# Large tiles on multiples of 512 bytes, and one of eight pairs of row blocks multiplied plainly, in a transformer layer's up projection

## The chip, the core and the metric

The kernel runs on one core of a Trainium2 chip. A core has five engines, each with its own queue of instructions: TensorE (PE: multiplications, and PEld: the loads of their stationary operand), VectorE (DVE), ScalarE (ACT), GpSimd (POOL) and SyncE (SP), which in this kernel issues nearly all DMAs. On-chip memory is SBUF, 128 partitions wide; TensorE writes its sums into the banks of PSUM. The metric is device time in microseconds (us) of one execution; the median of three runs is given.

## What is computed

One layer of a decoder, for 512 tokens of width 2048 in float32: an input projection, two groups of attention heads (a sliding window with sinks, and stick-breaking attention), an output projection, and an MLP with squared ReLU. The change lies in the MLP's first product, and in where tiles lie in memory:

```python
def reference(x, ..., w_out, norm_mlp_g, w_up, w_down):
    ...
        x = x + jnp.einsum('bse,ed->bsd', mix, w_out[l])
        h = rmsnorm(x, norm_mlp_g[l])
        u = jnp.einsum('bsd,df->bsf', h, w_up[l])          # 512 x 2048 by 2048 x 8192
        x = x + jnp.einsum('bsf,fd->bsd', jnp.square(jax.nn.relu(u)), w_down[l])
```

## The kernel before

**Precision.** Every large product is made of three multiplications. Each operand is split into `hi` (rounded, by a copy on ACT, line 89) and `lo` (the rest, by a subtraction on DVE, line 90), and hi x hi, hi x lo and lo x hi are added up in PSUM. `split` is the helper for this, so all splits show lines 89 and 90; `hi_u`, `lo_u` are those of the up projection's weights, `hi_d`, `lo_d` of the down projection's, `h2h`, `h2l` those of the normalized input `h`.

**The up projection** works through `w_up` in G = 32 groups of 256 columns. In each group it goes through KP = 8 pairs of row blocks (k = 0 to 7, 2 x 128 rows of `h`), so that 256 steps i = 8 g + k stand in a row. A pair is a product of 2 x 2 blocks: two blocks of 128 rows of weights by two blocks of 128 columns, and the tokens in two halves of HP = 256. It is made in Strassen's way (Winograd's form) with seven products in place of eight. Its sums of weights are made by POOL (`u_sums`, four operations on line 769 for the two pairs of one load), its sums of `h` once, by DVE, in `turn_x2` (line 744). Seven products of three multiplications with 256 columns are 21 a pair and 168 a group (lines 792 to 794: hi with `h2h`, hi with `h2l`, lo with `h2h`). The results gather in four PSUM banks; two sets of banks alternate by group.

**The steps around it.** `u_step(i)` asks on even i for the load of four pairs ahead and POOL's sums of two loads ahead, then splits the weights of step i + 2, multiplies step i, and lets one piece of `u_finish` of the group before go out. `u_finish` puts the four banks together (`p1`, `u`, `e`), applies ReLU (line 814) and square (816), makes the sums of activations that the down projection's own seven products want (`a`, lines 818 to 822), splits them (`ah` on ACT, line 825, 1792 columns; `al` on DVE, line 827) and writes both to memory (line 830). A scheduler puts the instructions of each engine in a fixed order from this; the queues work in that order.

**Group 0** is mixed with the end of the norm: `turn_x2` for pairs 6 and 7 stands between its steps. **The down projection** (lines 1023 to 1025) reads the written activations back as `ad`, its stationary operand, and takes 2688 multiplications of 512 columns. The three projections ahead (input with queries, keys and values, and output) go through line 114 to 116 with 832 multiplications each, of 512 columns.

**Where tiles lie.** Each pool of tiles takes its place in the order in which it is opened, from the left, or from the right edge of SBUF (`side="right"`). In the built program the weights' loads and their splits (`wst`, `whl`) start 384 bytes past a multiple of 512. The tiles of `big`, and later those of pairs 6 and 7 of `h2` and of `ew` in the same region, start 256 past, and all tiles from the right edge 480 past: `h2` of pairs 0 to 5, POOL's sums, `ad`, the loads of `w_down`. So the moving operand of the up projection is at 480 for k = 0 to 5 and at 256 for k = 6 and 7, its stationary one at 384; in the down projection the stationary `ad` is at 480, the moving weights at 384; in the projections ahead one operand is at 256, the other at 384.

Of the kernel before, what the change touches and what calls it, by code (L numbers as in the profile page):

```python
# [58 lines left out]
def hymba_layer(ctx: ExitStack, tc: tile.TileContext, x, norm_attn_g, w_in, q_norm_g, k_norm_g,  # L59
# [15 lines left out]
    odd, even, attn = ExitStack(), ExitStack(), ExitStack()  # L75
    big = {1: odd.enter_context(tc.tile_pool(name="big1", bufs=KD // 2)),
           0: even.enter_context(tc.tile_pool(name="big0", bufs=KD // 2))}
    once = attn.enter_context(tc.tile_pool(name="once", bufs=1, side="right"))
    qkp = attn.enter_context(tc.tile_pool(name="qkp", bufs=7, side="right"))
    vp = attn.enter_context(tc.tile_pool(name="vp", bufs=8, side="right"))  # L80
# [7 lines left out]
    def split(st, hi, lo):  # L88
        nc.scalar.copy(out=hi, in_=st)  # L89
        nc.vector.tensor_tensor(out=lo, in0=st, in1=hi.bitcast(F32), op=ALU.subtract)  # L90
# [268 lines left out]
        return o  # L359

    oscr = dram.tile([2 * 8, P, T], F32, name="oscr")
    S = [once.tile([P, T], F32, name=f"S{b}") for b in range(2)]

    def finish_o(av, branch, c, keep=False):
# [325 lines left out]

    HP = T // 2
    KP = KD // 2
    G = DFF // 256
    x2scr = dram.tile([4, P, NT, 512], F32, name="x2scr")
    ss2 = const.tile([P, NT, 4], F32, name="ss2")
# [33 lines left out]
    def turn_x2(n, kk, banks):  # L731

        k = 2 * n + kk
        hq = xw.tile([P, 8, HP], F32, tag="hq", bufs=2, name=f"hq{k}")
        for r in range(2):
            tr = banks.tile([P, 512], F32, tag="pa" if banks is pa else "pp", name=f"x2t{k}{r}")
            c0 = (2 * kk + r) * P
            for t in range(NT):
                nc.tensor.transpose(tr[:, t * P:(t + 1) * P], xts[n, t][:, c0:c0 + P], ident)
            g = gT[:, 16 + 2 * k + r:17 + 2 * k + r]  # L740
            nc.scalar.mul(out=hq[:, 0::7] if r == 0 else hq[:, 1:3],
                          in_=tr.rearrange("p (b t) -> p b t", b=2), mul=g)
        for o, a, b in ((3, 7, 0), (4, 2, 3), (5, 2, 7), (6, 1, 4)):
            nc.vector.tensor_tensor(out=hq[:, o], in0=hq[:, a], in1=hq[:, b], op=ALU.subtract)
        hi = hp[k].tile([P, 7, HP], F32R, name=f"h2h{k}")
        lo = hp[k].tile([P, 7, HP], F32R, name=f"h2l{k}")
        split(hq[:, 0:7], hi, lo)
        h2[k] = hi, lo


# [10 lines left out]
    def u_sums(i):  # L761
        if i < G * KP // 2:
            w = raws[i]
            s_ = sp.tile([P, 2, 4, P], F32, tag="s", name=f"s_u{i}")
            for o, a, b, op in ((s_[:, :, 0], w[:, :, 0], w[:, :, 2], ALU.add),
                                (s_[:, :, 2], w[:, :, 1], w[:, :, 0], ALU.subtract),
                                (s_[:, :, 1], s_[:, :, 0], w[:, :, 1], ALU.subtract),
# [3 lines left out]

    def u_split(i):
        if i < G * KP:
            w, s_ = raws[i // 2][:, i % 2], sums[i // 2][:, i % 2]
            hi = whl.tile([P, 7, P], F32R, tag="hi", name=f"hi_u{i}")
            lo = whl.tile([P, 7, P], F32R, tag="lo", name=f"lo_u{i}")
            split(w[:, 1:4], hi[:, 0:3], lo[:, 0:3])
            split(s_, hi[:, 3:7], lo[:, 3:7])
            parts_u[i] = hi, lo


    U_PRODUCTS = ((0, 0, 0, 0), (2, 1, 1, 0), (1, 6, 3, 1), (3, 3, 2, 0), (5, 5, 2, 1), (4, 4, 1, 1), (6, 2, 3, 0))

    def u_products(i, ps):
        g, k = divmod(i, KP)
        (wh, wl), (hh, hl) = parts_u.pop(i), h2[k]
        begun = set()
        for a, b, n, half in U_PRODUCTS:
            o = ps[n][:, half * HP:(half + 1) * HP]
            first = k == 0 and n not in begun  # L790
            begun.add(n)
# [6 lines left out]
    def u_finish(g, ps, ew):  # L798
# [11 lines left out]
        yield  # L810
        nc.vector.tensor_tensor(out=e[:, 0:4:2], in0=u, in1=z, op=ALU.add)
        nc.vector.tensor_tensor(out=e[:, 3], in0=u[:, 1], in1=y[:, 0], op=ALU.add)
        a = ew.tile([P, 8, HP], F32, tag="a", name=f"a{g}")
        nc.scalar.activation(out=a[:, 0:4], in_=e[:, 0:4], func=AF.Relu)
        yield
# [243 lines left out]
```

## Time and profile before

| | |
|---|---|
| median of three runs | 2077.21 us (2077.02 to 2078.11) |
| the profiled execution | 2076.19 us, span of its instructions 2074.5 us |
| TensorE busy | 2019.0 us, 97% of the span, 11652 multiplications |
| DVE, ACT, POOL busy | 1678.5, 1008.1, 1045.7 us |
[...]

A time in the trace is counted from the span's start. In a timeline, a multiplication's row begins where it begins; since they overlap in the engine, what one costs is the distance from its start to the next one's, not its own length. In a row of windows the first two numbers are its ends, and an engine's number in parentheses is how many records touch the window, so those that began shortly ahead of it are among them. A row of waits gives the engine and line that waited, after the arrow whom for, then the total, how often, and the longest.

### The profile page before, as it was taken

The page shows a single profiled execution, that of the slowest core. Times are in us where ns is not written, and L with a number is a line of the kernel's source. Part 1 is how long each engine was busy: PE and PEld are TensorE (multiplying, and loading weights), DVE is VectorE, ACT ScalarE, POOL GpSimd, SP SyncE. Part 2 cuts the span into 40 slices and gives each one's busy share as a digit, 9 for nine tenths or more (in the row PEclk, how much of TensorE's full clock was granted, in tenths as well). Part 3 has the DMA queues.
Part 4 walks back from the last instruction along what each step waited for, and adds up shares of the span by engine and source line. Part 5 has one row for each costly group of instructions (what it writes and reads, how often), then busy time and mean ns, then how long its engine had stood idle before and what let it go on. Part 6 is the DMA issues. An engine that isn't in the chain of part 4 may idle for free. (4 is left out here: it accounts for less than half of the span.)

```text
span 2074.5 us, 30963 instructions
## 1 busy us (share of the span) xinstructions
PE 2019.0 (97%) x11652; PEld 1722.1 (83%) x11652; DVE 1678.5 (81%) x2038; ACT 1008.1 (49%) x1692; POOL 1045.7 (50%) x904
## 2 busy tenths in 40 slices
PE   8999999999999999999999999998999999999998
PEld 7777777777677889999999999997788888888876
DVE  4468646565775579999999999998889888988999
ACT  6267534544553565555555555554543333333332
POOL 0013322222220137777778787877755555555663
PEclk9999999999999999999999999999999999999999
DMA  6742332223345535656555555658756456456453
GB/s 217 116 133 82 102 96 73 72 92 117 103 140 175 180 109 163 195 186 194 187 188 194 185 196 184 198 183 326 265 208 230 158 206 244 144 204 260 152 187 108
DMA packets 213913, 350.28 MB, mean 169 GB/s; under 512 B 9779, under 2 KB 154372, under 8 KB 206596
## 3 DMA queue, kind: packets, MB, share of 16 engines
q1 hardware_dynamic: 211216, 345.02, 49.1%
q10 hardware_dynamic: 2548, 3.30, 1.4%
q8 instruction: 91, 1.49, 0.3%
q14 instruction: 58, 0.48, 0.1%
HBM read 270.16 MB, written 78.12 MB: 168 GB/s over the span
## 5 line engine op out<-in xcount | busy, mean ns | idle before, releaser
L794 PE MATMUL ps_u<-h2h,lo_u 128*128 128x256 f32 x1792 | 506.7, 283 | 15.7 <-DVE lo_u L90 15.7
L793 PE MATMUL ps_u<-h2l,hi_u 128*128 128x256 f32 x1792 | 506.4, 283 | 2.7 <-DVE h2l L90 2.7
L792 PE MATMUL ps_u<-h2h,hi_u 128*128 128x256 f32 x1792 | 506.3, 283 | 0.6 <-ACT h2h L89 0.6
L769 POOL TENSOR_TENSOR s_u<-st_u 128x256 f32<-128x256 f32 x256 | 254.6, 1015 | 242.3 <-DVE lo_u L90 171.7
L1024 PE MATMUL ps_d<-lo_d,ad 128*128 128x512 f32 x896 | 357.1, 399 | 6.4 <-DVE lo_d L90 6.4
L1023 PE MATMUL ps_d<-hi_d,ad 128*128 128x512 f32 x896 | 356.5, 398 | 6.5 <-DMA ad<-ac 4.9
L794 PEld LDWEIGHTS ps_u<-h2h,lo_u 128*128 128x128 f32 x1792 | 340.1, 190 | 21.9 <-DVE lo_u L90 21.8
L1025 PE MATMUL ps_d<-hi_d,ad 128*128 128x512 f32 x896 | 356.5, 398 | 0.0
L793 PEld LDWEIGHTS ps_u<-h2l,hi_u 128*128 128x128 f32 x1792 | 337.0, 188 | 3.2 <-DVE h2l L90 3.1
L792 PEld LDWEIGHTS ps_u<-h2h,hi_u 128*128 128x128 f32 x1792 | 336.6, 188 | 1.0 <-ACT h2h L89 1.0
L90 DVE TENSOR_TENSOR lo_d<-T,hi_d 128x1024 fp32r<-128x1024 f32 x128 | 244.8, 1924 | 49.4 <-ACT hi_d L89 49.4
L89 ACT CAST hi_u<-s_u 128x512 fp32r<-128x512 f32 x256 | 158.3, 618 | 226.4 <-POOL s_u L769 226.4
L918 POOL TENSOR_TENSOR T<-st_d,T 128x1024 f32<-128x1024 f32 x64 | 162.6, 2543 | 208.9 <-DVE lo_d L90 207.7
L90 DVE TENSOR_TENSOR lo_u<-s_u,hi_u 128x512 fp32r<-128x512 f32 x256 | 248.0, 969 | 8.6 <-ACT hi_u L89 8.4
L89 ACT CAST hi_d<-T 128x1024 fp32r<-128x1024 f32 x128 | 134.3, 1051 | 214.0 <-PE ps_d L1025 196.8
L1024 PEld LDWEIGHTS ps_d<-lo_d,ad 128*128 128x128 f32 x896 | 169.4, 189 | 49.9 <-DVE lo_d L90 8.9
L1023 PEld LDWEIGHTS ps_d<-hi_d,ad 128*128 128x128 f32 x896 | 169.6, 189 | 48.8 <-ACT a L816 4.9
L90 DVE TENSOR_TENSOR lo_u<-st_u,hi_u 128x384 fp32r<-128x384 f32 x256 | 202.3, 790 | 4.6 <-ACT hi_u L89 4.6
L1025 PEld LDWEIGHTS ps_d<-hi_d,ad 128*128 128x128 f32 x896 | 169.6, 189 | 41.1
L90 DVE TENSOR_TENSOR lo_d<-st_d,hi_d 128x1024 fp32r<-128x1024 f32 x96 | 190.1, 1996 | 13.3 <-ACT hi_d L89 13.2
L89 ACT CAST hi_d<-st_d 128x1024 fp32r<-128x1024 f32 x96 | 100.9, 1051 | 163.5 <-PE ps_d L1025 163.5
L769 POOL TENSOR_TENSOR s_u<-s_u,st_u 128x256 f32<-128x256 f32 x128 | 140.5, 1098 | 0.0
(220 smaller groups left out, 3823.6 us busy)
## 6 DMA issues: line engine op xcount, KB each, us to landing
st_u<-in_w_up SPq DMA_DIRECT2D x128, 512.0 KB, 4.4
st_d<-in_w_down SPq DMA_DIRECT2D x64, 1024.0 KB, 6.1
ad<-ac SPq DMA_DIRECT2D x56, 1024.0 KB, 6.4
ac<-ah SPq DMA_DIRECT2D x32, 896.0 KB
ac<-al SPq DMA_DIRECT2D x32, 896.0 KB, 4.8
st_qk<-in_w_in SPq DMA_DIRECT2D x64, 256.0 KB, 3.0
st_o<-in_w_out SPq DMA_DIRECT2D x32, 512.0 KB, 4.2
st_qa<-in_w_in SPq DMA_DIRECT2D x16, 512.0 KB, 3.8
```

What stands on the lines that cost most here:

```text
L89: nc.scalar.copy(out=hi, in_=st)
L90: nc.vector.tensor_tensor(out=lo, in0=st, in1=hi.bitcast(F32), op=ALU.subtract)
L769: nc.gpsimd.tensor_tensor(out=o, in0=a, in1=b, op=op)
L792: nc.tensor.matmul(o, wh[:, a], hh[:, b], start=first, stop=False, skip_group_check=True)
L793: nc.tensor.matmul(o, wh[:, a], hl[:, b], start=False, stop=False, skip_group_check=True)
L794: nc.tensor.matmul(o, wl[:, a], hh[:, b], start=False, stop=(k == KP - 1), skip_group_check=True)
L918: nc.gpsimd.tensor_tensor(out=o, in0=raw[cj, a, h], in1=raw[cj, b, h], op=ALU.subtract)
L1023: nc.tensor.matmul(o, al, bh[:, kk], start=first, stop=False, skip_group_check=True)
L1024: nc.tensor.matmul(o, al, bl[:, kk], start=False, stop=False, skip_group_check=True)
L1025: nc.tensor.matmul(o, ar, bh[:, kk], start=False, stop=end, skip_group_check=True)
```

## The change

Two things are changed.

**Placement.** Three tiles are added that nothing reads: 128 bytes a partition among the constants, 128 in the pool of small tiles, 480 at the right edge. In the built program every large tile then starts on a multiple of 512 bytes.

**Pair 7 of each group plainly.** For k = `PLAIN` = 7, the four blocks of weights and the four of `h` are used as they are: eight products, 24 multiplications and not 21. POOL makes no sums of weights for it (the four operations of the last load have half the columns), and its weights are split by one operation of 512 columns on ACT and on DVE, where there were two, of 384 and 512. In `turn_x2` the four subtractions fall away for it, and its split has 1024 columns, not 1792. One of the eight results goes to a half bank that had been unused, and `u_finish` adds it with one DVE operation more (the line after the former 812).

```diff
+    edge = ctx.enter_context(tc.tile_pool(name="edge", bufs=1, side="right"))
+    edge.tile([P, 120], F32, name="pad_right")
...
+    const.tile([P, 32], F32, name="pad_left")
+    sm.tile([P, 32], F32, tag="pad", bufs=1, name="pad_small")
...
+    PLAIN = KP - 1
...
-            nc.scalar.mul(out=hq[:, 0::7] if r == 0 else hq[:, 1:3],
+            nc.scalar.mul(out=hq[:, 1:3] if r else hq[:, 0:4:3] if k == PLAIN else hq[:, 0::7],
                           in_=tr.rearrange("p (b t) -> p b t", b=2), mul=g)
...
+        nb = 4 if k == PLAIN else 7
+        hi = hp[k].tile([P, nb, HP], F32R, name=f"h2h{k}")
+        lo = hp[k].tile([P, nb, HP], F32R, name=f"h2l{k}")
+        if k != PLAIN:
+            for o, a, b in ((3, 7, 0), (4, 2, 3), (5, 2, 7), (6, 1, 4)):
+                nc.vector.tensor_tensor(out=hq[:, o], in0=hq[:, a], in1=hq[:, b], op=ALU.subtract)
+        split(hq[:, 0:nb], hi, lo)
...
             s_ = sp.tile([P, 2, 4, P], F32, tag="s", name=f"s_u{i}")
+            if i % (KP // 2) == PLAIN // 2:
+                w, s_ = w[:, 0:1], s_[:, 0:1]
...
+            parts_u[i] = hi, lo
+            if i % KP == PLAIN:
+                split(w, hi[:, 0:4], lo[:, 0:4])
+                return
+            s_ = sums[i // 2][:, i % 2]
             split(w[:, 1:4], hi[:, 0:3], lo[:, 0:3])
             split(s_, hi[:, 3:7], lo[:, 3:7])
...
+    U_PLAIN = ((1, 0, 1, 0), (3, 1, 1, 0), (1, 3, 3, 0), (3, 2, 3, 0), (0, 0, 3, 1), (2, 1, 3, 1), (0, 3, 0, 1),
+               (2, 2, 0, 1))
...
-        for a, b, n, half in U_PRODUCTS:
+        for a, b, n, half in U_PLAIN if k == PLAIN else U_PRODUCTS:
...
         nc.vector.tensor_tensor(out=e[:, 3], in0=u[:, 1], in1=y[:, 0], op=ALU.add)
+        nc.vector.tensor_tensor(out=e[:, 3], in0=e[:, 3], in1=w[:, 1], op=ALU.add)
```

The scheduler's order changes with it. The first place is DVE near the end of a usual group (group 11, whose pair 7 is step 95; `al10` belongs to group 10, `lo_u96` to pair 0 of group 12). Before:

```order
L90 TENSOR_TENSOR lo_u94_10148<-st_u47_9939,hi_u94_10147 128x384
L90 TENSOR_TENSOR lo_u94_10148<-s_u47_10076,hi_u94_10147 128x512
L827 TENSOR_TENSOR al10_10206<-a10_10110,ah10_10205 128x1792
L90 TENSOR_TENSOR lo_u95_10177<-st_u47_9939,hi_u95_10176 128x384
L90 TENSOR_TENSOR lo_u95_10177<-s_u47_10076,hi_u95_10176 128x512
L90 TENSOR_TENSOR lo_u96_10216<-st_u48_10007,hi_u96_10215 128x384
```

and now:

```order
L92 TENSOR_TENSOR lo_u94_10172<-st_u47_9959,hi_u94_10171 128x384
L92 TENSOR_TENSOR lo_u94_10172<-s_u47_10099,hi_u94_10171 128x512
L837 TENSOR_TENSOR a10_10134<-a10_10134 128x256
L840 TENSOR_TENSOR a10_10134<-a10_10134 128x256
L92 TENSOR_TENSOR lo_u95_10201<-st_u47_9959,hi_u95_10200 128x512
L845 TENSOR_TENSOR al10_10228<-a10_10134,ah10_10227 128x1792
L92 TENSOR_TENSOR lo_u96_10238<-st_u48_10030,hi_u96_10237 128x384
```

The split of step 95 is one operation, and it has moved ahead of `al10`; two of the sums `a10` that stood ahead of `lo_u94` now stand behind it.

The second place is DVE in group 0, around the splits of `h2` for pairs 6 and 7 (`hq` holds the sums of `h`, `lo_u8` is the first step of group 1). Before:

```order
L90 TENSOR_TENSOR h2l6_7129<-hq6_7111,h2h6_7128 128x1792
L744 TENSOR_TENSOR hq7_7159<-hq7_7159 128x256 x3
L90 TENSOR_TENSOR lo_u7_7215<-st_u3_6925,hi_u7_7214 128x384
L744 TENSOR_TENSOR hq7_7159<-hq7_7159 128x256
L90 TENSOR_TENSOR lo_u7_7215<-s_u3_7079,hi_u7_7214 128x512
L90 TENSOR_TENSOR lo_u8_7249<-st_u4_7016,hi_u8_7248 128x384
L90 TENSOR_TENSOR lo_u8_7249<-s_u4_7182,hi_u8_7248 128x512
L90 TENSOR_TENSOR h2l7_7177<-hq7_7159,h2h7_7176 128x1792
```

and now:

```order
L92 TENSOR_TENSOR h2l6_7131<-hq6_7117,h2h6_7130 128x1792
L92 TENSOR_TENSOR lo_u7_7217<-st_u3_6931,hi_u7_7216 128x512
L92 TENSOR_TENSOR h2l7_7179<-hq7_7165,h2h7_7178 128x1024
L92 TENSOR_TENSOR lo_u8_7249<-st_u4_7022,hi_u8_7248 128x384
L92 TENSOR_TENSOR lo_u8_7249<-s_u4_7184,hi_u8_7248 128x512
```

The four subtractions are gone, and `h2l7` stands ahead of both operations of `lo_u8`.

The third place is SP's queue at the step into the down projection, where `ad00` is the first activation that it reads back. Before, and in the same sequence now, with other buffer numbers:

```order
L830 DMA ac7_6220<-ah30_15574 128x7x256
L830 DMA ac7_6220<-al30_15575 128x7x256
L901 DMA st_d001_15640<-in_w_down 128x2x1024
L909 DMA ad00_15642<-ac0_6213 128x2048
L901 DMA st_d010_15656<-in_w_down 128x2x1024
```

```order
L848 DMA ac7_6226<-ah30_15636 128x7x256
L848 DMA ac7_6226<-al30_15637 128x7x256
L919 DMA st_d001_15705<-in_w_down 128x2x1024
L927 DMA ad00_15707<-ac0_6219 128x2048
L919 DMA st_d010_15721<-in_w_down 128x2x1024
```

Nothing moved here: the load of `ad00` is queued behind the write of `al30`.

## Rows read from the trace of the kernel before

**Rows 1.** The page's totals: busy us, share of the span, instructions.
```profile
PE 2019.0 (97%) x11652; PEld 1722.1 (83%) x11652; DVE 1678.5 (81%) x2038; ACT 1008.1 (49%) x1692; POOL 1045.7 (50%) x904
```

**Rows 2.** Windows: ends, length, busy us (records) of PE, PEld, DVE, ACT, POOL; clock; DMA.
```profile
748.19:775.82 27.63, 24.29 (x185) 23.50 (x184) 23.77 (x32) 17.96 (x34) 13.49 (x12) 0.94 0.31 96
775.82:1400.83 625.01, 610.71 (x5043) 604.77 (x5041) 599.51 (x750) 349.63 (x600) 480.77 (x479) 1.00 0.58 188
1400.83:1427.46 26.63, 20.52 (x170) 20.14 (x169) 22.11 (x29) 12.97 (x20) 16.70 (x13) 1.00 0.69 248
1458.82:2020.86 562.04, 562.04 (x2400) 451.85 (x2399) 499.57 (x388) 218.93 (x218) 328.12 (x120) 1.00 0.55 203
```

**Rows 3.** Waits of PE, 735 to 1423 us: total, times, longest.
```profile
PE ps_u L794 <- DVE lo_u L90: 15.7, 30, 1.4
PE ps_u L793 <- DVE h2l L90: 2.7, 2, 1.7
```

**Rows 4.** Timeline of DVE at the end of group 11: start, length, instruction.
```profile
999.33 2.56 DVE L827 TENSOR_TENSOR al<-a,ah 128x1792 fp32r<-128x1792 f32 x1
1001.81 0.55 DVE L90 TENSOR_TENSOR lo_u<-st_u,hi_u 128x384 fp32r<-128x384 f32 x1
1002.28 0.68 DVE L90 TENSOR_TENSOR lo_u<-s_u,hi_u 128x512 fp32r<-128x512 f32 x1
1002.88 0.55 DVE L90 TENSOR_TENSOR lo_u<-st_u,hi_u 128x384 fp32r<-128x384 f32 x1
1003.35 1.22 DVE L90 TENSOR_TENSOR lo_u<-s_u,hi_u 128x512 fp32r<-128x512 f32 x1
```

**Rows 5.** Timeline of PE there, pair 7.
```profile
1001.65 0.28 PE L793 MATMUL ps_u<-h2l,hi_u 128*128 128x256 f32 x1
1002.41 0.38 PE L794 MATMUL ps_u<-h2h,lo_u 128*128 128x256 f32 x1 [0.48 <-DVE lo_u L90]
1002.63 0.28 PE L792 MATMUL ps_u<-h2h,hi_u 128*128 128x256 f32 x1
```

**Rows 6.** Windows: pairs 0-5, pairs 6-7, a whole group, input projection, output projection.
```profile
775.82:790.94 15.12, 15.12 (x128) 15.12 (x127) 12.98 (x19) 7.76 (x14) 12.09 (x13) 1.00 0.35 105
790.94:795.93 4.99, 4.99 (x44) 4.99 (x43) 4.24 (x5) 3.98 (x6) 3.55 (x3) 1.00 0.60 193
...
963.09:983.92 20.83, 20.36 (x170) 20.15 (x169) 20.04 (x26) 11.65 (x20) 16.04 (x17) 1.00 0.59 192
283.92:325.29 41.37, 41.37 (x180) 33.53 (x178) 11.80 (x11) 10.81 (x13) 7.54 (x6) 1.00 0.33 101
657.07:685.41 28.34, 28.34 (x123) 22.98 (x122) 9.67 (x11) 10.88 (x19) 0.00 (x0) 1.00 0.66 224
```

**Rows 7.** Groups of DVE instructions, 963.09 to 983.92: count, busy, mean ns, idle before.
```profile
L90 DVE TENSOR_TENSOR lo_u<-s_u,hi_u 128x512 fp32r<-128x512 f32 x8 | 7.8, 976 | 0.3 <-ACT hi_u L89 0.3
L90 DVE TENSOR_TENSOR lo_u<-st_u,hi_u 128x384 fp32r<-128x384 f32 x9 | 7.4, 821 | 0.0
...
L818 DVE TENSOR_TENSOR a<-a 128x256 f32<-128x256 f32 x1 | 0.4, 424 | 0.5 <-ACT a L816 0.5
...
L812 DVE TENSOR_TENSOR e<-u,ps_u 128x256 f32<-128x256 f32 x1 | 0.4, 409 | 0.0
```

**Rows 8.** Timeline of DVE in group 0.
```profile
770.13 0.55 DVE L90 TENSOR_TENSOR lo_u<-st_u,hi_u 128x384 fp32r<-128x384 f32 x1
770.60 0.68 DVE L90 TENSOR_TENSOR lo_u<-s_u,hi_u 128x512 fp32r<-128x512 f32 x1
771.42 2.34 DVE L90 TENSOR_TENSOR h2l<-hq,h2h 128x1792 fp32r<-128x1792 f32 x1
```

**Rows 9.** Timelines of SP's queue and of PE at the step down.
```profile
1417.60 0.37 SPq L830 DMA_DIRECT2D ac<-al  x1
1418.02 0.68 SPq L901 DMA_DIRECT2D st_d<-in_w_down  x1
1418.75 1.24 SPq L909 DMA_DIRECT2D ad<-ac  x1
...
1427.46 0.47 PE L1023 MATMUL ps_d<-hi_d,ad 128*128 128x512 f32 x1 [4.68 <-DMA ad<-ac]
```

More of the change, by code (lines that the diff above doesn't have):

```diff
@@ L740, in turn_x2 @@
             g = gT[:, 16 + 2 * k + r:17 + 2 * k + r]
-            nc.scalar.mul(out=hq[:, 0::7] if r == 0 else hq[:, 1:3],
+            nc.scalar.mul(out=hq[:, 1:3] if r else hq[:, 0:4:3] if k == PLAIN else hq[:, 0::7],
                           in_=tr.rearrange("p (b t) -> p b t", b=2), mul=g)
[L743 to L747, printed above, removed]
+        nb = 4 if k == PLAIN else 7
[5 more added lines that the diff above has]
+        split(hq[:, 0:nb], hi, lo)
         h2[k] = hi, lo
@@ L773, in u_split @@
         if i < G * KP:
-            w, s_ = raws[i // 2][:, i % 2], sums[i // 2][:, i % 2]
+            w = raws[i // 2][:, i % 2]
             hi = whl.tile([P, 7, P], F32R, tag="hi", name=f"hi_u{i}")
             lo = whl.tile([P, 7, P], F32R, tag="lo", name=f"lo_u{i}")
+            parts_u[i] = hi, lo
[3 more added lines that the diff above has]
+            s_ = sums[i // 2][:, i % 2]
             split(w[:, 1:4], hi[:, 0:3], lo[:, 0:3])
             split(s_, hi[:, 3:7], lo[:, 3:7])
-            parts_u[i] = hi, lo
+    U_PLAIN = ((1, 0, 1, 0), (3, 1, 1, 0), (1, 3, 3, 0), (3, 2, 3, 0), (0, 0, 3, 1), (2, 1, 3, 1), (0, 3, 0, 1),
+               (2, 2, 0, 1))
     U_PRODUCTS = ((0, 0, 0, 0), (2, 1, 1, 0), (1, 6, 3, 1), (3, 3, 2, 0), (5, 5, 2, 1), (4, 4, 1, 1), (6, 2, 3, 0))
```

## The prediction

> **What bounds the kernel now.** I read the page's totals first, then busy time by stretch, then TensorE's waits, then the timelines of one pass of the up projection. TensorE is busy for 97% of the span [rows 1], so time is won where it waits or where one multiplication follows another more slowly than it could. The up projection's 32 column groups fill about a third of the run: 27.63 us for group 0, 625.01 us for groups 1 to 30, 26.63 us for group 31 with the step into the down projection [rows 2]. A usual group takes 20.83 us. In it, 168 multiplications follow each other without a gap except at one place [rows 3 to 5]. There are 30 waits for `lo_u`, one in each group from 2 on. The place is the third multiplication of row-block pair k=7, the first that reads `lo`: its predecessor starts at 1001.65, it starts at 1002.41, and the next one at 1002.63. The DVE rows say why: `al` of the group before ran from 999.33 for 2.56 us, and both `lo` operations of k=7 stand behind it. Against two steps of 0.12 us that costs about 0.74 us a group.
>
> The second thing is the step from one multiplication to the next. Group 1 has no such wait, so it shows the steps cleanly [rows 6]: its pairs k=0 to 5 are 126 multiplications in 15.12 us (the window counts two more, still draining when it opens), 120.0 ns each; its pairs 6 and 7 are 42 in 4.99 us, 118.8 ns each. The work is of one shape; what differs is where the moving operand lies: `h2` of pairs 0 to 5 starts 480 bytes past a multiple of 512, that of pairs 6 and 7 256 bytes past. With 512 columns I find the same. A run of 178 multiplications of the input projection (operands at 256 and 384) takes 41.37 us, 232.4 ns each, and 122 of the output projection 28.34 us, 232.3 ns [rows 6]; the down projection, whose stationary `ad` lies at 480, takes 562.04 us for 2399 without a longer gap, 234.3 ns each [rows 2]. So 480, the only offset that is no multiple of 64, goes with 1.2 to 1.9 ns more; between 256 and 384 there is nothing to see.
>
> **The eighth product.** Pair 7 gets eight products for seven, three multiplications each: 3 x 118.8 = 0.36 us a group, all on TensorE's path, 11.4 us in 32 groups. What it takes away is on DVE, ACT and POOL. The split of k=7 is one operation of 512 columns for one of 384 and one of 512: DVE loses one of mean 0.82 us a group [rows 7]. POOL's four sums of the last load are made for one pair and not two, an eighth of its 16.04 us [rows 6]. DVE gains one addition from PSUM over 256 columns; its nearest row is L812 of the same form, 0.41 us [rows 7].
>
> **The order on DVE.** This decides more than the counts. In the changed program `lo` of k=7 stands ahead of `al`. DVE came to `al` at 999.33 and TensorE needed `lo` at 1001.77 (1001.65 and one step). One `lo` of 512 columns takes 0.68 us alone and 1.22 beside POOL [rows 4], and the new addition 0.41: ready 0.8 to 1.4 us before it is wanted, and the wait goes. What is late next? Behind `al` now stands `lo` of the next group's k=0. Before, it was ready at 1002.88 + 0.55 = 1003.43, and TensorE came to it about 1005.0 (18 steps after 1002.63 to the group's end, then two more): 1.6 us spare. Between the same neighbours DVE now does 0.60 to 1.15 + 2.48 us for 3.55 (999.33 to 1002.88), 0 to 0.45 less, and TensorE arrives 0.74 - 0.36 = 0.38 us sooner: 1.2 to 1.7 us stay spare. Over the whole group DVE must fit as well: 20.04 us busy now [rows 6], less 0.82, plus 0.41, is 19.63; its idle time of 0.3 and 0.5 us [rows 7] makes 20.43. From this comes off what POOL's lighter load gives back. A `lo` has a mean of 0.98 or 0.82 us against 0.68 or 0.55 alone, 0.57 us for the two, 4.5 us over eight pairs; an eighth less POOL is some 0.6 us. So DVE needs about 19.9 us where TensorE needs 171 x 118.8 = 20.31. I take TensorE as the bound, by a small margin.
>
> **The placement.** 128 bytes in the constants, 128 in the small pool and 480 at the right edge put every large tile on a multiple of 512. No trace of before shows an operand there. Its cost a multiplication lies between that of the multiples of 64 (118.8 and 232.4 ns, the nearest rows) less another step of 1.2 to 1.9 ns, should a whole boundary count, and the present value plus such a step, should equal offsets of both operands hurt. I take the nearest rows: 120.0 to 118.8 for pairs 0 to 5, 234.3 to 232.4 for the down projection, nothing for the projections before (their operands lie at 256 and 384 already). For DMAs, DVE, ACT and POOL I put nothing: TensorE waits for no load inside the up projection [rows 3]. If that cover were gone, the shortest spare time above, 1.2 us, is what a late load would first use up.
>
> [...]
>
> **Sum, against the profiled execution's own 2076.19 us (span 2074.5), 1.0 below the median of 2077.21.** Groups 1 to 30: 30 x 20.31 = 609.3 for 625.0, -15.7. Group 0: TensorE waits twice for `h2l`, 2.7 us with 1.7 the longer [rows 3]; the shorter one, 1.0, is for pair 7, where `h2l` of 1792 columns stands behind two `lo` of the next group [rows 8]; now it has 1024 columns and stands ahead of them, so -1.0, +0.36 for the product, -0.15 for 126 faster steps, -0.8. Group 31 and the step down: 0, although its wait goes too, because the down projection starts when `ad` lands at 1427.46, 4.7 us after TensorE fell idle. `ad` is queued on SP behind the write of `al` (1417.60) and a weight load (1418.02) [rows 9]; both queues keep this order, and `al` is made no earlier. TensorE then waits longer for the same landing; I allow 1 us either way. Down projection: 2688 x 1.9 = -5.1. Together -21.6: about 2055 on the median.
>
> **Rivals.**
> - *Placement gives nothing* (the 1.2 and 1.9 ns have another cause, such as the part of memory or the kind of stage, or tiles do not land where intended). For it: within one stage I have two sets of operands only. Against it: the same sign and size in two stages, once on the moving and once on the stationary side. Then a group is 15.12 + 45 x 0.1188 = 20.47: -10.8, group 0 -0.6, total -11.4: 2066.
> - *DVE becomes the bound*, the wait moving to the head of the next group, behind `al`. For it: DVE's 20.43 without any relief is over 20.31, and POOL may now work through `al`'s 2.6 us, where it used to wait. Against it: the spare times above. Between 20.43 and the old 20.83 a group: 2059 to 2071, middle 2065.
> - *A whole boundary is worth a second step.* For it: operands at 256 or 384 still cross one boundary more than those at 0 will. Against it: 256 and 384 don't differ. 5472 x 1.2 = 6.6 and (2688 + 2496 of the three projections) x 1.9 = 9.8 more: 2039.
> - *Slower: equal offsets.* Now both operands of a multiplication start at the same offset in 512 bytes, which no stage before had (384 with 480 or 256, 480 with 384). If that costs a step above today's in place of one below: a group is 171 x 121.2 = 20.72, -3.2 in 30; group 0 -0.5; down +5.1, the other projections' 2496 x 1.9 = +4.7: +6, 2083. It decides from about 1 ns a multiplication on (11.4 us over 10,700). Nothing in the rows speaks for it.
>
> **How the numbers follow.** Forecast 0.60 (2050 to 2060: 1 us for the step down, some 2 us for group 0 and stretches at the lower clock, 0.2 ns on a step), placement nothing 0.12, DVE 0.14, second step 0.09, equal offsets 0.05. Predicted 2055. The range takes the forecast, the first rival and most of DVE's, and on the low side half a second step: 2045 to 2068. A measurement of this kernel can tell about 0.2% (4 us) from no change. Faster by more than that: 0.93 (all but the last and a sliver of DVE's upper end); within it 0.02; slower 0.05.
>
> **What would show it.** A window over groups 1 to 30 should be near 609 us, and TensorE's waits should no longer list `lo_u` 30 times: right for the order. If they list it at the first pair of a group, it is DVE. The step of pairs 0 to 5 should read 118.8 ns and that of the down projection 232.4: right for the placement; 120.0 and 234.3 are the first rival, 117.5 and 230.5 the second step, 121 and 236 equal offsets. TensorE's wait for `ad` should grow by over 1 us while its landing keeps its place after the start of group 31. I would be wrong altogether if the three projections ahead, which I price at nothing, change their time by several us.

## The result, and the profile after

The changed kernel takes 2044.4 us (2044.0 to 2044.6, four runs) where the kernel before took 2077.7 in the same session: a ratio of 0.984, with a 95% interval of 0.982 to 0.986, or 33.3 us less. The forecast of 2055 had the sign; the time lies 0.6 us under the forecast's range of 2045 to 2068.

The profiled execution took 2044.01 us, with a span of 2042.0 for 2074.5. Where the 32.5 us came from, stage by stage (each stage ends where the next one's first multiplication starts):

| stage | before, us | after, us | moved | predicted |
|---|---|---|---|---|
| all up to the up projection | 748.2 | 741.8 | -6.4 | 0 |
| group 0 | 27.63 | 24.85 | -2.8 | -0.8 |
| groups 1 to 30 | 625.01 | 615.60 | -9.4 | -15.7 |
| group 31 and the step down | 26.63 | 25.94 | -0.7 | 0 |
| down projection to the end | 647.0 | 633.8 | -13.2 | -5.1 |

The windows that answer to [rows 2] and [rows 6], from the trace after (columns as there): the first three are group 0, groups 1 to 30, and group 31 with the step down; then one whole group, and the six pairs k = 0 to 5 of it; then 178 multiplications of the input projection, 2399 of the down projection, and ahead of those its first 98.

```profile
741.83:766.68 24.85, 22.75 (x189) 22.34 (x188) 20.45 (x30) 17.66 (x34) 11.60 (x13) 1.00 0.38 115
766.68:1382.28 615.60, 615.60 (x5133) 615.60 (x5132) 538.26 (x750) 349.28 (x570) 459.80 (x482) 1.00 0.59 192
1382.28:1408.22 25.94, 20.67 (x173) 20.50 (x172) 18.29 (x27) 12.18 (x18) 10.02 (x9) 0.95 0.66 243
971.88:992.40 20.52, 20.52 (x174) 20.52 (x173) 17.94 (x26) 11.65 (x19) 15.33 (x17) 1.00 0.59 193
...
971.88:987.00 15.12, 15.12 (x129) 15.12 (x128) 12.54 (x20) 9.53 (x15) 12.10 (x15) 1.00 0.45 151
...
279.51:319.89 40.38, 40.38 (x179) 33.42 (x178) 11.91 (x11) 10.83 (x13) 7.55 (x6) 1.00 0.35 104
...
1443.82:1987.62 543.80, 543.80 (x2401) 450.26 (x2399) 503.92 (x387) 219.47 (x218) 323.85 (x119) 1.00 0.56 207
1408.22:1443.82 35.60, 26.97 (x98) 21.03 (x98) 28.73 (x16) 13.50 (x15) 25.59 (x10) 0.84 0.98 394
```

In groups 1 to 30 TensorE is busy for all of 615.60 us: 30 x 171 multiplications at 120.0 ns, and no gap. Pairs 0 to 5 take 15.12 us for 126, 120.0 ns each, just what they took before. With 512 columns the step fell instead: 40.38 us for 178 is 226.9 ns (232.4 before), 543.80 for 2399 is 226.7 (234.3 before). TensorE's four longest waits from the up projection to the start of the down projection (735 to 1460 us) are now:

```profile
PE ps_d L1041 <- DMA ad<-ac: 5.3, 1, 5.3
PE ps_d L1042 <- DVE lo_d L92: 4.2, 1, 4.2
PE ps_d L1041 <- ACT hi_d L91: 2.8, 1, 2.8
PE ps_u L810 <- DVE h2l L92: 1.8, 1, 1.8
```

The 30 waits for `lo_u` [rows 3] are gone, and one of the two for `h2l`. DVE at the end of group 11, the place that answers to [rows 4]:

```profile
984.27 1.22 DVE L92 TENSOR_TENSOR lo_u<-st_u,hi_u 128x512 fp32r<-128x512 f32 x1
986.15 2.02 DVE L845 TENSOR_TENSOR al<-a,ah 128x1792 fp32r<-128x1792 f32 x1 [0.66 <-ACT ah L843]
988.10 1.10 DVE L92 TENSOR_TENSOR lo_u<-st_u,hi_u 128x384 fp32r<-128x384 f32 x1
```

`lo` of pair 7 is ready at 985.49; TensorE comes to that pair at 971.88 + 147 x 0.12 = 989.52, 4 us later.

### The profile page after: what moved, and what is told of

Read it like the earlier page. It is cut to its first block, busy times and chain, and to the rows that moved or that the text cites. A ratio compares the mean times of both kernels' runs of the same rounds, so it can differ in the third digit from the quotient of the medians.

```text
span 2042.0 us, 31119 instructions
## 1 busy us (share of the span) xinstructions
PE 1996.6 (98%) x11748; PEld 1732.2 (85%) x11748; DVE 1614.2 (79%) x2034; ACT 1007.8 (49%) x1660; POOL 1012.9 (50%) x904
## 5 line engine op out<-in xcount | busy, mean ns | idle before, releaser
L809 PE MATMUL ps_u<-h2h,hi_u 128*128 128x256 f32 x1824 | 516.4, 283 | 0.3 <-ACT h2h L91 0.3
L1041 PE MATMUL ps_d<-hi_d,ad 128*128 128x512 f32 x896 | 350.6, 391 | 9.7 <-DMA ad<-ac 5.3
L810 PEld LDWEIGHTS ps_u<-h2l,hi_u 128*128 128x128 f32 x1824 | 350.2, 192 | 2.1 <-DVE h2l L92 2.0
L809 PEld LDWEIGHTS ps_u<-h2h,hi_u 128*128 128x128 f32 x1824 | 350.2, 192 | 0.5 <-ACT h2h L91 0.5
L811 PEld LDWEIGHTS ps_u<-h2h,lo_u 128*128 128x128 f32 x1824 | 350.2, 192 | 0.0
L1043 PE MATMUL ps_d<-hi_d,ad 128*128 128x512 f32 x896 | 350.1, 391 | 0.0
L779 POOL TENSOR_TENSOR s_u<-st_u 128x256 f32<-128x256 f32 (+1 forms) x256 | 200.2, 801 | 251.9 <-DVE lo_u L92 180.8
L91 ACT CAST hi_u<-st_u 128x384 fp32r<-128x384 f32 (+1 forms) x256 | 134.0, 523 | 221.9 <-PE ps_u L810 144.8
L92 DVE TENSOR_TENSOR lo_u<-st_u,hi_u 128x384 fp32r<-128x384 f32 (+1 forms) x256 | 196.5, 768 | 20.1 <-ACT hi_u L91 20.1
L92 DVE TENSOR_TENSOR lo_u<-s_u,hi_u 128x512 fp32r<-128x512 f32 x224 | 177.6, 793 | 0.4 <-ACT hi_u L91 0.3
L779 POOL TENSOR_TENSOR s_u<-st_u,s_u 128x256 f32<-128x256 f32 (+1 forms) x128 | 167.4, 1308 | 10.0
```

Source lines behind the costliest of these rows:

```text
L779: nc.gpsimd.tensor_tensor(out=o, in0=a, in1=b, op=op)
L809: nc.tensor.matmul(o, wh[:, a], hh[:, b], start=first, stop=False, skip_group_check=True)
L810: nc.tensor.matmul(o, wh[:, a], hl[:, b], start=False, stop=False, skip_group_check=True)
L811: nc.tensor.matmul(o, wl[:, a], hh[:, b], start=False, stop=(k == KP - 1), skip_group_check=True)
L1041: nc.tensor.matmul(o, al, bh[:, kk], start=first, stop=False, skip_group_check=True)
L1043: nc.tensor.matmul(o, ar, bh[:, kk], start=False, stop=end, skip_group_check=True)
```

## The experiments

### Which property of the place sets the step

The prediction read the step from each operand's own offset. Two theories stood after the result. **B**: starting on a multiple of 512 is what helps. **E**: what counts is how the starts of the two operands of one multiplication stand to each other; after the change they are equal. Three kernels ran beside the changed one.

`micro` has streams of multiplications alone, nothing of the layer, 36 for each pair of starts:

```python
for t in range(12):
    ws = slice(8 * w + 128 * (t % 4), 8 * w + 128 * (t % 4) + 128)   # stationary, 32 w bytes on
    ms = slice(8 * m, 8 * m + cols)                                  # moving, 32 m bytes on
    for i, (a, b) in enumerate((("wh", "mh"), ("wh", "ml"), ("wl", "mh"))):
        nc.tensor.matmul(ps[:, 0:cols], ops[a][:, ws], ops[b][:, ms], ...)
```

> Only streams of multiplications in the hi/hi, hi/lo, lo/hi pattern, 36 for each pair of start offsets of the moving and the stationary operand within 512 bytes, first with 256 and then with 512 columns; nothing of the layer is computed, the input is copied to the output. Theory B (each operand pays for the 512-byte boundaries that it crosses): with 512 columns the step is shortest with both at 0, about 226.7 ns, in between with one of them at 0, about 229 to 230, and 232.4 with neither. Theory E (what counts is that both start at the same offset): 226.7 wherever the two offsets are equal, 256/256 as 0/0, and 232 or more elsewhere. With 256 columns both theories must give 120.0 at 0/0, 120.0 at moving 480 and stationary 384, and 118.5 at 256 and 384, as the two kernels' traces have them.

Measured: both starts alone, and multiples of 512, tell nothing; the distance does, the stationary operand's start less the moving one's, modulo 256 bytes. At one distance the step, after a stream's first steps, was the same wherever the pair lay, with few exceptions: three of the 16 streams at 64 bytes with 256 columns ran at 117.8 ns to their end and not at 113.3 (one of them is shown under "Two rates at one distance"), and one of the four at 224 bytes at 117.8 and not at 116.7. Windows of 30 steps each (busy PE, PEld, ACT, POOL; clock; DMA), the moving operand 64 bytes past a multiple of 512, at distances of 0, 64, 128 and 192 bytes, first with 256 columns, then with 512:

```profile
47.12:50.72 3.60, 3.60 (x33) 3.60 (x32) 0.00 (x0) 0.00 (x0) 1.00 0.23 79
51.42:54.82 3.40, 3.40 (x32) 3.40 (x31) 0.00 (x0) 0.00 (x0) 1.00 0.00 0
55.52:59.08 3.56, 3.56 (x32) 3.56 (x31) 0.00 (x0) 0.00 (x0) 1.00 0.00 0
59.79:63.33 3.54, 3.54 (x33) 3.54 (x32) 0.00 (x0) 0.00 (x0) 1.00 0.02 5
406.55:413.35 6.80, 6.80 (x32) 5.63 (x30) 0.00 (x0) 0.00 (x0) 1.00 0.00 0
414.74:421.74 7.00, 7.00 (x31) 5.64 (x30) 0.00 (x0) 0.00 (x0) 1.00 0.00 0
423.14:430.10 6.96, 6.96 (x31) 5.65 (x30) 0.00 (x0) 0.00 (x0) 1.00 0.01 2
431.49:438.36 6.87, 6.87 (x32) 5.64 (x31) 0.00 (x0) 0.00 (x0) 1.00 0.00 0
```

A thirtieth of each length is the step: 120.0, 113.3, 118.7 and 118.0 ns with 256 columns, 226.7, 233.3, 232.0 and 229.0 with 512. So equal starts are the best place for 512 columns, and for 256 the worst (beside 160 bytes). The steps of before follow: distances of 160 bytes (384 less 480) in pairs 0 to 5, where the one stream at that distance gave 120.0 and the layer 120.0; 128 in pairs 6 and 7 and in the projections ahead (118.7 and 232.2, the layer 118.8 and 232.4); 96 in the down projection (one stream, 234.3, the layer 234.3). The streams at 160 bytes with 256 columns and at 96 bytes with 512, 30 steps each:

```profile
280.28:283.88 3.60, 3.60 (x32) 3.60 (x31) 0.00 (x0) 0.00 (x0) 1.00 0.00 0
896.62:903.65 7.03, 7.03 (x32) 5.65 (x31) 0.00 (x0) 0.00 (x0) 1.00 0.01 2
```

`all_256` moves every large tile to 256 past a multiple of 512, so the starts are equal and none is on such a multiple:

```diff
-    edge.tile([P, 120], F32, name="pad_right")
+    edge.tile([P, 56], F32, name="pad_right")
...
-    const.tile([P, 32], F32, name="pad_left")
+    const.tile([P, 96], F32, name="pad_left")
```

> The changed kernel with other pads, so that every large tile starts 256 bytes past a multiple of 512. Theory B: both operands cross boundaries again, steps 232.4 ns with 512 columns and 118.5 with 256: the down projection gives back 13 us, the projections 6, the groups gain 171 x 1.5 ns = 0.26 us each, whole about 2055 us. Theory E: as the changed kernel, 226.7 and 120.0 ns, 2044 us.

Measured: 2044.8 us (2043.1 to 2046.5), the changed kernel's time; step 120.0 in the up projection, 226.7 in the down projection. B falls.

### The two parts of the change, one at a time

`plain_only` has no added tiles; `place_only` has them and seven products for every pair (`PLAIN = -1`, and without the addition of `w[:, 1]`).

> The changed kernel without its three pads: pair 7 plain, tiles where they were before. If the two parts add up and the steps between multiplications belong to the placement alone, the groups of the up projection take 126 x 120.0 + 45 x 118.5 = 20.45 us without a wait for lo_u, the projections ahead and the down projection stay as before, and the whole is about 2077.7 - 11.5 - 2 = 2064 us. If the plain pair also changed steps elsewhere, it would be below 2058.

> The kernel before with the three pads alone: seven products for pair 7. By the trace of the changed kernel the projections ahead lose about 6 us and the down projection 13, and the up projection's step is 120.0 ns for all pairs, so that a group is 168 x 120.0 = 20.16 us plus its wait for lo_u of about 0.7: about 20.85, no gain there. Whole: about 2057 us. If the wait went with the placement too (DVE or POOL faster on the new offsets), groups would be 20.2 us and the whole 2038.

Measured: 2069.0 us for the plain pair alone (ratio 0.996, 0.995 to 0.998), 8.0 less than the 2077.0 of before in that session; 2051.4 for the placement alone (0.988, 0.986 to 0.990), 25.6 less. Added up that is 33.6, and both together gave 33.3. One usual group and groups 1 to 30 of each, first `place_only`, then `plain_only`:

```profile
934.81:955.66 20.85, 20.41 (x170) 20.21 (x169) 20.08 (x26) 11.64 (x20) 16.07 (x17) 1.00 0.59 189
768.33:1393.58 625.25, 612.18 (x5042) 606.29 (x5041) 600.01 (x750) 349.50 (x600) 481.10 (x479) 1.00 0.58 188
```

```profile
938.85:959.30 20.45, 20.45 (x173) 20.45 (x172) 17.95 (x26) 11.66 (x19) 15.25 (x17) 1.00 0.58 194
775.20:1388.90 613.70, 613.70 (x5133) 613.70 (x5132) 538.52 (x750) 349.58 (x570) 455.30 (x480) 1.00 0.59 192
```

So the placement does nothing for the up projection: 625.25 us for 625.01. All of its gain lies in the stages with 512 columns. The plain pair alone brings groups 1 to 30 to 613.70 us, 1.9 less than the changed kernel, where pairs 6 and 7 went from a step of 118.8 to one of 120.0.

Both times missed what was expected by 5 to 6 us, `plain_only` above it and `place_only` below it, and the place is the same: the start of the down projection. Its first 98 multiplications, first `place_only`, then `plain_only` (31.36 us before, 35.60 in the changed kernel, both below):

```profile
1420.67:1451.22 30.55, 25.82 (x98) 19.81 (x98) 28.74 (x14) 12.90 (x15) 26.03 (x8) 0.91 1.03 415
1414.85:1451.11 36.26, 28.32 (x97) 21.76 (x98) 28.38 (x16) 13.43 (x15) 25.82 (x10) 0.83 0.98 389
```

So it is the plain pair that loses some 5 us there, not the placement.

### What sets a group's time

`up_64` is the changed kernel with the up projection's stationary tiles 64 bytes on, at the distance with the shortest step, `up_128` with 128 bytes; `up_64_seven` is `place_only` with 64.

```diff
-            hi = whl.tile([P, 7, P], F32R, tag="hi", name=f"hi_u{i}")
+            hi = whl.tile([P, 912], F32R, tag="hi", name=f"hi_u{i}")[:, 16:].rearrange("p (a b) -> p a b", b=P)
```

(and the same for `lo`; 928 and 32 for 128 bytes.)

> The changed kernel, with the up projection's stationary tiles starting 64 bytes further on (their buffers have the room), all else as it is. Theory E (the step hangs on the distance between the two operands' starts, modulo 256 bytes; 64 bytes gave 113.4 ns in the streams of multiplications alone, 0 gave 120.0): step 113.4, groups 1 to 30 near 582 us for 615.6, 2010 us in all. Rival D (DVE, busy 17.9 us of a group's 20.5, is then the bound): PE waits for lo_u in every group, a group stays over 20 us, 2025 to 2035 us. Rival O (in the whole kernel the other engines' traffic sets the step): step 120, 2044 us.

> The same 64 bytes, with seven products for every pair and the pads (the kernel place_only, 2051.4 us, with the shift). Theory E: 5376 steps of 6.5 ns less, 35 us, so 2016 us, if the wait for lo_u of 14.5 us stays as it is. Rival D: the wait for lo_u grows to 1 us or more a group, 2030 us or more. Against the kernel with the shift and the plain pair this tells what the plain pair is worth at the shorter step: 32 x 3 x 0.113 = 10.9 us of products against the waits.

> The changed kernel with the up projection's stationary tiles 128 bytes further on: the distance that pairs 6 and 7 had before. Theory E: step 118.6 (as in the streams alone, and for those pairs before), 5472 x 1.4 ns = 7.7 us less than the changed kernel, 2037 us. A theory by which any inequality of the two starts helps alike: as with 64 bytes, 2010. Rival O: 2044.

Measured: `up_64` 2038.4 us (2035.2 to 2039.9; ratio 0.981, 0.979 to 0.982), `up_64_seven` 2054.2 (2052.1 to 2054.9), `up_128` 2038.8 (2036.4 to 2044.0). The mean step was 114.1, 114.0 and 118.8 ns, near what E has; in the first two it is a mean of stretches at 113.3 and stretches at 117.8. But only `up_128` got what the step gives, 171 x 118.65 = 20.29 us a group, and that up to group 24. `up_64` ran groups 1 to 3 at the full gain, and usual ones not (first group 2, then group 8):

```profile
785.73:805.11 19.38, 19.38 (x174) 19.38 (x173) 17.45 (x25) 11.65 (x19) 14.90 (x16) 1.00 0.57 184
905.24:925.68 20.44, 19.74 (x174) 19.55 (x172) 18.51 (x27) 11.46 (x20) 15.24 (x17) 1.00 0.59 193
```

TensorE's waits in its up projection (735 to 1400 us), and the two groups of DVE's instructions in 780 to 1340 us that had nearly all of DVE's idle time ahead of them (28 and 27 instructions; the last number is the idle time, with what ended it):

```profile
PE ps_u L811 <- DVE lo_u L92: 15.5, 23, 0.7
```

```profile
L845 DVE TENSOR_TENSOR al<-a,ah 128x1792 fp32r<-128x1792 f32 x28 | 56.7, 2026 | 18.6 <-ACT ah L843 18.6
...
L836 DVE TENSOR_TENSOR a<-a 128x256 f32<-128x256 f32 x27 | 17.5, 647 | 31.2 <-ACT a L834 31.2
```

One of TensorE's waits, at the first pair of group 9, which starts at 925.68 (the `lo_u` that it waits for started at 925.61, right behind `al`):

```profile
926.76 0.38 PE L811 MATMUL ps_u<-h2h,lo_u 128*128 128x256 f32 x1 [0.69 <-DVE lo_u L92]
```

DVE is busy 18.51 us of a group of 20.44, and 31.2/27 + 18.6/28 = 1.82 us more go to two waits for ACT, for its square and for `ah`, both made from what DVE itself made shortly before; together 20.33. DVE's round, with its two waits for ACT, is the bound here, and it needs 20.4 us. With seven products it needs 20.85: `up_64_seven` takes that at a step of 114.0 ns, `place_only` at 119.9, and the kernel before needs 20.83 [rows 6]. The window of groups 1 to 30 of `up_64_seven`, 625.00 us, is before's 625.01 to the hundredth, with TensorE busy 23 us less:

```profile
767.94:1392.94 625.00, 587.64 (x5043) 580.75 (x5041) 599.57 (x750) 349.69 (x600) 480.87 (x479) 1.00 0.59 188
```

So rival D of these expectations held, with `up_64` 3 us over the range given for it. The kernel before was bound in its groups by DVE's round, not by TensorE, and the plain pair takes 0.4 us off that round.

`up_128` shows the same round from the other side. Its groups of 20.29 us are 0.1 to 0.2 shorter than DVE's round; TensorE's first wait for `lo_u` comes in group 25, and groups 25 to 28 take 20.35 to 20.65. From group 28 on the step is 120.0 ns at the same distance. Groups 1 to 30, then group 29:

```profile
769.37:1379.30 609.93, 609.93 (x5132) 609.66 (x5131) 551.38 (x746) 347.38 (x570) 453.12 (x478) 1.00 0.59 191
1338.26:1358.78 20.52, 20.52 (x173) 20.52 (x172) 18.61 (x27) 11.51 (x20) 15.25 (x16) 1.00 0.60 193
```

### A second plain pair

If so, more plain pairs pay as long as TensorE stays under the round. `two_plain` is the changed kernel with k = 3 and k = 7 plain, `up_64_two` has the 64 bytes besides.

```diff
-    PLAIN = KP - 1
+    PLAIN = (KP // 2 - 1, KP - 1)
...
-            if i % (KP // 2) == PLAIN // 2:
+            if i % 2:
```

(and `in PLAIN` for `== PLAIN`.)

> The changed kernel with two plain pairs and no shift (step 120.0). If TensorE alone sets its groups, as its 20.52 = 171 x 120.0 says, a group becomes 174 x 120.0 = 20.88 us and the whole 31 x 0.36 = 11 us slower than the changed kernel, 2055 us. If VectorE has a hand in it, less than that: 2044 us or under.

> The shift of 64 bytes with two of the eight pairs plain (k = 3 and 7): 174 multiplications a group. Theory D2 (with the shift, VectorE's round of one group, 20.43 us without a pause of its own making, sets the pace; the first plain pair took 0.41 us off that round, of which 0.42 us for its added sum had to come off first, so a second, which adds none, takes 0.83 us off): VectorE's round 19.6 us, TensorE's 174 x 113.4 = 19.73 us, a group 19.7 to 19.8, 2017 us. Rival (the pace of 20.43 comes from the loads of weights, or from GpSimd): a group stays at 20.4 us, 2038 us or above.

Measured: `two_plain` 2050.8 us (2050.0 to 2053.1; ratio 0.988, 0.986 to 0.989), a group 20.88 = 174 x 120.0: with TensorE as the bound the three multiplications cost their 0.36 us. (The profiled execution is 9.0 us over the changed kernel's: 30 x 0.36 = 10.8, less 1.5 in group 0 and 0.3 elsewhere.) `up_64_two` gave 2015.8, 2018.5, 2040.4 and 2042.5 us in its four executions (ratio 0.979, 0.973 to 0.985). Groups 1 to 30 of the profiled one, and of `up_64_two_pool` (below), which has the same groups:

```profile
764.43:1356.03 591.60, 591.60 (x5223) 591.60 (x5222) 503.84 (x721) 337.33 (x540) 351.19 (x481) 1.00 0.62 200
```

```profile
764.01:1378.81 614.80, 614.80 (x5222) 614.80 (x5221) 513.88 (x721) 336.78 (x540) 345.05 (x482) 1.00 0.60 193
```

TensorE waits nowhere in either. The first runs at 591.60/5220 = 113.3 ns a step, as expected, and so at 19.72 us a group, with the same loads of weights: these did not set the pace. (POOL's sums fell together with DVE's splits, so its part in DVE's round is not told apart.) The second runs at 117.8, 20.49 us. 5568 steps of 4.45 ns are 24.8 us, about what lies between the two pairs of times above; the slower pair itself has no trace. In group 0 both run at 117.8; after its wait of 0.8 us for `h2l` the one goes on at 113.3, the other at 117.8, and each holds it for 31 groups.

### Two rates at one distance

`stops` has streams of 42 multiplications, each behind a ScalarE copy into the stationary tile.

```python
nc.scalar.copy(out=ops["wh"][:, 8 * w:8 * w + c], in_=st[:, 8 * w:8 * w + c])   # c = 16, 32, ... columns
```

> Streams of 42 multiplications alone (the input is copied to the output, nothing of the layer is computed), each behind a short stop of TensorE: a ScalarE copy into the stationary tile, of 16 to 384 columns, that must wait for the stream before. 24 streams of 256 columns for each of the distances 0, 64, 128 and 192 bytes, 12 of 512 columns for 0 and 128. With the shift of 64 bytes the layer's step was 113.4 ns in one execution and 117.8 in another, each held for 31 groups. Theory P (at some distances two rates are possible, and a stop chooses between them): among the 24 streams at 64 bytes both 113.4 and 117.8 appear, at 0 only 120.0, and 226.8 at 512 columns. Rival T (one rate for a distance, and the layer's second rate comes from the other engines' traffic): all 24 at 113.4.

Measured, over the last 24 steps of each stream: at 0 bytes 120.0 in 23 of 24 (148.8 in the first, which began with steps of 213), at 64 bytes 113.3 in all 24, at 128 118.5 to 118.7 in all, at 192 bytes 113.3 in 9 and 117.8 in 15; with 512 columns 226.7 at 0 and 232.1 to 232.6 at 128, in all 12. Two streams in a row at 192 bytes, 30 steps each (columns as for `micro`):

```profile
408.97:412.37 3.40, 3.40 (x32) 3.40 (x31) 0.08 (x1) 0.00 (x0) 1.00 0.00 0
413.97:417.50 3.53, 3.53 (x32) 3.53 (x31) 0.10 (x1) 0.00 (x0) 1.00 0.00 0
```

So there are distances with two rates, and a stream keeps its rate. That much of theory P holds. P named 64 bytes, and there these streams had one rate, as T says; but three of the 16 streams of `micro` at 64 bytes had the other one. One of them, 30 steps:

```profile
148.88:152.41 3.53, 3.53 (x32) 3.53 (x31) 0.00 (x0) 0.00 (x0) 1.00 0.00 0
```

That is the rate of 117.8 ns (3.53 us by 30, rounded), with no other engine at work and no stop of TensorE ahead of it. So the second rate does not need the other engines' traffic, and rival T falls; nor does it need a stop. What decides which of the two rates follows, in a stream or in the layer, stays open.

### The step into the down projection

The changed kernel's first 98 multiplications there take 35.60 us (above), against this window of before:

```profile
1427.46:1458.82 31.36, 26.63 (x98) 20.38 (x98) 29.56 (x15) 13.32 (x15) 25.19 (x8) 0.89 1.03 412
```

TensorE is idle in it 8.6 us, not 4.7, and busy 0.3 us longer although its step is shorter, the granted clock being 0.84 for 0.89. DVE and POOL in the trace after:

```profile
1411.34 2.59 DVE L836 TENSOR_TENSOR a<-a 128x256 f32<-128x256 f32 x1
1413.86 2.62 DVE L839 TENSOR_TENSOR a<-a 128x256 f32<-128x256 f32 x1
1416.40 2.61 DVE L837 TENSOR_TENSOR a<-a 128x256 f32<-128x256 f32 x1
1419.04 2.50 DVE L840 TENSOR_TENSOR a<-a 128x256 f32<-128x256 f32 x1
```

```profile
1413.62 2.58 POOL L936 TENSOR_TENSOR T<-st_d,T 128x1024 f32<-128x1024 f32 x1
1416.16 2.57 POOL L936 TENSOR_TENSOR T<-st_d,st_d 128x1024 f32<-128x1024 f32 x1
```

The last group's four sums, 0.4 to 1.0 us each in a usual group, advance one for one with POOL's sums `T`, and take 10.2 us. Why they do is not shown. Before, three of the four ran ahead of POOL's sums; the first and the last of them in that trace:

```profile
1427.33 0.43 DVE L818 TENSOR_TENSOR a<-a 128x256 f32<-128x256 f32 x1 [2.27 <-ACT a L816]
1433.95 2.60 DVE L822 TENSOR_TENSOR a<-a 128x256 f32<-128x256 f32 x1
```

`plain_only` has waits of TensorE there like the changed kernel's (4.2 us for `lo_d`, 2.1 for `hi_d`); in `place_only` one of the four is stretched as before (2.61 us, the others 0.41 to 0.69). `step_pool` gives these four to POOL:

```diff
+        sums = nc.gpsimd if g == G - 1 else nc.vector
-        nc.vector.tensor_tensor(out=a[:, 4], in0=a[:, 0], in1=a[:, 3], op=ALU.add)
+        sums.tensor_tensor(out=a[:, 4], in0=a[:, 0], in1=a[:, 3], op=ALU.add)
...
```

> The changed kernel with the four sums of activations of the last group alone made by GpSimd and not by VectorE. Theory S (at the step into the down projection these four, 0.42 us each elsewhere, took 2.5 to 2.6 us each because they alternate with GpSimd's sums T, which held the cast ah, the casts of hi_d queued behind it on ScalarE, and TensorE for 7.9 us): four GpSimd sums of about 1.1 us, ah some 5 us earlier, TensorE's waits between 1421 and 1429 us fall to 3 or 4 us, 2040 us. Rival (the casts wait for the loads of w_down or for T itself, which now comes 4.3 us later on GpSimd): no gain, 2044 to 2048 us.

> The same, and the last group's four sums on GpSimd, as in step_pool, which was some 3.5 us faster than the changed kernel: 2013 us if the two gains add up, 2017 if the step into the down projection is filled by something else at this pace.

Measured: `step_pool` 2041.3 us (2040.9 to 2043.4), 3 less than the changed kernel; the sums take 0.74 us each on POOL, TensorE's waits for `lo_d` and `hi_d` fall from 7.0 to 3.1 us (1400 to 1460 us), and from the first multiplication of the down projection to the end it is 630.5 us for 633.8. S holds. `up_64_two_pool` took 2036.1 us (2035.5 to 2039.3; ratio 0.981, 0.979 to 0.982). By their times all four executions belong with the slower pair of `up_64_two`, some 5 us under it, and the profiled one had the step of 117.8. If the other three had it too, which no trace shows, the gain adds up; the 2013 us did not come.

## Why the prediction was right or wrong

**The step of the working that failed** is the one that put the difference of 1.2 and 1.9 ns down to each operand's own offset, and so priced the placement at -5.1 us in the down projection and at nothing in the three projections ahead; the runs showed -13.2 and -6.4 there, from the distance between the two operands' starts.

**The order on DVE, right as far as the changed kernel goes.** The wait for `lo_u` went, from all 30 groups, and no wait at the head of the next group took its place. Whether the order did it is not shown: no run has the plain pair with the old order, and a round that is 0.4 us shorter, beside TensorE's 20.52, would do it too. With the new order and a shorter step, in `up_64`, the wait is back at the head of the next group, behind `al`: the place that the second rival named. **The eighth product** costs its 0.36 us where TensorE is the bound (20.88 less 20.52 with a second plain pair).

**What a group was bound by, wrong.** The prediction took the groups for TensorE's, held up at one place. The other reading stood in the same trace. DVE was busy for 20.04 of 20.83 us and idle only behind ACT, 0.3 and 0.5 us [rows 6, 7]. That these add up to the round shows nothing, for every engine's do. But of the waits that the trace lists in the 20 groups from 963.09 to 1379.90 us not one is for TensorE; ACT's and POOL's waits for another engine are these (total, times, longest):

```profile
ACT hi_u L89 <- POOL s_u L769: 146.2, 40, 5.1
POOL s_u L769 <- DVE lo_u L90: 89.3, 40, 3.0
```

So the round of DVE, ACT and POOL ran by itself, with DVE hardly ever idle, and the wait for `lo_u` was only TensorE's slack against it. In the changed kernel, over 20 groups from 971.88 us on, ACT does wait for TensorE:

```profile
ACT hi_u L91 <- PE ps_u L810: 92.6, 68, 1.8
```

That a step 6 ns shorter left the 20.85 us as they were shows what bound them. The prediction's own 20.43 us for DVE after the change is what `up_64` measured, but by luck in its parts: DVE was busy for 18.51 us and not 19.63, so that more relief came than the 0.5 us allowed for POOL's lighter load, while the waits for ACT grew from 0.8 to 1.8 us. What made either is not shown. Had the step been 118.8, TensorE's 20.31 would have lain under DVE's 20.4, and yet little would have come of the second rival: `up_128` has that step, waits only from group 25 on, and needs 609.93 us for groups 1 to 30 where the prediction had 609.3.

**The placement in the up projection, wrong.** The step is 120.0 ns, not 118.8, in all pairs: 171 x 1.2 ns x 30 = 6.2 us, the whole of what groups 1 to 30 fall short (-9.4 for -15.7).

**The placement in the down projection, mis-sized.** 234.3 to 226.7 ns is 7.6 a multiplication, not 1.9: 2688 x 7.6 = -20.4 for -5.1. Of this 7 us were given back, some 5 at its start (35.60 for 31.36, although 98 steps should give 0.7 there) and 2 at its end. The 5 are a cost of the plain pair (36.26 in `plain_only`, 30.55 in `place_only`) that the prediction put at nothing: it had looked at that start only for `ad`; the stretched sums stood on no list.

**The three projections ahead, priced at nothing, wrong.** They have 512 columns and went from a distance of 128 to 0, and -6.4 us came of it. This is the point from which, as the prediction said, it would be wrong altogether. At 226.7 ns all along it would have been 14 us. But in the trace after, the step falls to 226.7 only from the eleventh step of an unbroken run on (the first ten take 234.0 to 227.8 in the mean), and the attention's own multiplications end most runs after ten: the mean is 228.5 for 232.5 before, some 9 us. Another 1.5 went to the lower clock, by a stretch that moved into this stage (see group 0).

**Why that step failed.** It took each operand's own offset, 480 being no multiple of 64, for the cause. In the same rows the distance of the two operands changed with it (160 against 128 bytes, 96 against 128), and nothing there told the two readings apart. The bounds were drawn from that reading, one step of 1.9 ns up or down, and so left out the 5.7 ns that equal starts gave. The last rival had the right variable, equal starts, and the wrong sign: it counted them as a loss with both sizes; with 256 columns they are a worst place, by up to 6.7 ns, with 512 the best. The first rival, that the placement gives nothing, is contradicted by `place_only` with 25.6 us. In the streams of `micro`, with no other engine at work, the step goes from 113.3 to 120.0 ns with the distance between the two starts.

**Group 0**, -2.8 for -0.8: the wait for `h2l` of pair 7 went, as predicted (2.7 us in two to 1.8 in one). The rest is the clock. Before, the granted clock was 0.94 in this window [rows 2], after 1.00: 3.4 us at a granted clock of 0.51 had lain at 769.0, and lie at 620.7 us after:

```profile
620.70:624.10 3.40, 3.40 (x10) 2.63 (x9) 3.40 (x5) 0.95 (x2) 0.21 (x1) 0.51 0.59 196
```

`step_pool`, the same program up to there, has such a stretch in group 0:

```profile
742.39:768.72 26.33, 24.23 (x188) 23.82 (x187) 21.28 (x30) 17.66 (x34) 13.01 (x15) 0.94 0.40 121
```

So 1.3 us are the change's and 1.5 the clock's. **Group 31 and the step down**, -0.7 for 0: the wait for `ad` grew by 0.6 us, not by over 1, and `ad` landed 0.7 us sooner after the start of group 31.

The two large misses had opposite signs, 6.3 us too much and 17.2 too little; only their difference shows in the total.

## What to carry to other kernels

When two stages of one shape differ in their step, list all that differs between their operands, the distance of the two starts among it, before giving the step a cause; a short kernel of multiplications alone settles most of it, and its answer holds for one number of columns only (here 113.3 ns at 64 bytes was the shortest step with 256 columns, 226.7 at 0 with 512). And an engine that is 97% busy need not be the bound: list who waits for whom over some usual rounds. If no engine waits for that one, the others' round sets the pace: shortening the first engine's steps then gives nothing (`up_64_seven`: 625.00 us for 625.01), and moving work off the others' round does (`up_64`: a group in 20.44 us for 20.85). A run that changes the steps alone shows it. Last, look at the seams: a gain in steady stretches can be given back where the stages' queues meet (here some 5 us at the start of the down projection).

## What the runs showed of the hardware

- The step of float32 multiplications in the split form used here hangs on the distance of the stationary operand's start from the moving one's, modulo 256 bytes: 113.3 to 120.0 ns with 256 columns, 226.7 to 234.3 with 512 (`micro`), and the two sizes have their best places apart (64 and 0 bytes).
- At one distance two rates can be stable: 113.3 and 117.8 ns at 64 bytes (`micro`, `up_64`) and at 192 (`stops`), 118.7 and 120.0 at 128 (`up_128`). In `up_64_two` the rate changed from 117.8 to 113.3 ns at a wait of TensorE of 0.8 us, and was then kept, without a stop, over 31 groups; in `up_128` it was 118.7 at first and 120.0 from group 28 on. Groups 1 to 30 of `up_64_two` and `up_64_two_pool` lie 23 us apart by it; that it also parts the executions of `up_64_two`, by 24 us, fits their times and is not shown by a trace.
- At the step into the down projection of the changed kernel four short DVE sums advanced one for one with POOL's long ones: 2.5 to 2.6 us each, where the first of them, ahead of POOL's sums, took 0.43 before.
